# Sliding windows on one core: second halves of the split stores alternate with whole ones, and the copies without shuffle run on ScalarE

## Chip, cores, metric

One core of one Trainium2 chip. The metric is device time in microseconds (us) of one execution, as the median of several; all runs told here are in the fast state (one core, granted clock 1.0 in every profile). The profile's span is about 2 us shorter than the device time; where a sum is made from the profile, it is compared with the span. The sets of runs were made on different chips, so each is compared with the kernel before in its own rounds (196.74 to 197.01 us).

## The reference

```python
x: float32 [16, 64, 64, 64]; window_size = 8; stride = 4      # batch, c, h, w
n_h = n_w = 15
for i in range(n_h):
    for j in range(n_w):
        result[:, i, j] = x[:, :, 4*i : 4*i + 8, 4*j : 4*j + 8]   # [16, 64, 8, 8]
# result: float32 [16, 15, 15, 64, 8, 8]
```

Nothing is computed. 16.8 MB are read and 59 MB are written.

## The kernel before

x lies in one tile `L` with 128 partitions: 16 batches x 2 channel halves x 4 bands of 16 rows. A "window" in the code is one column position `j` and one row position `s` of a band, for all 128 partitions together. It is gathered into a slot of the ring `G` and stored by an indirect DMA that GpSimd (POOL) issues, since the output rows are scattered. For `s == 3` half of the rows come from the next band; a shuffle brings them over. The first 12 windows are stored in two halves of 16 channels, so that stores can begin when half of x is loaded.

```python
    UNITS = 18                                   # half slots in the ring
    G = gpool.tile([P, UNITS * HCL, WS, WS], f32, name="G")
    def window(j, s, half):
        ...
        g = G[:, u * HCL : (u + n) * HCL, :, :]
        if not last:
            nc.vector.tensor_copy(out=g, in_=L[:, cs, s * ST : s * ST + WS, cols])
        else:
            nc.vector.tensor_copy(out=g[:, :, 0:ST, :], in_=L[:, cs, s * ST : RB, cols])
            nc.vector.stream_shuffle(out=g[:, :, ST:WS, :], in_=L[:, cs, 0:ST, cols], mask=nxt)
        ...
        st = nc.gpsimd.indirect_dma_start(out=o, out_offset=..., in_=g..., ...)

    order = [(j, s) for j in range(NW) for s in range(NSLOT)]     # 60 windows
    EARLY = 12
    for half in range(2):
        for j, s in order[:EARLY]:
            window(j, s, half)
    for j, s in order[EARLY:]:
        window(j, s, None)
```

That makes 24 half stores and 48 whole ones. `idx_h` and `idx_hlast` in the profile are the halves, `idx` and `idx_last` the whole ones, "last" being those with a shuffle.

## Time and profile before

| | before |
|---|---|
| median (lowest to highest) | 196.94 us (196.81 to 197.00) |
| span of the profile | 194.9 us |
| DMA engines busy, 65 to 75 us | 0.83 |
| rate, 65 to 75 us | 338 GB/s |
| rate, 100 to 175 us | 409 GB/s |
| POOL from the first second-half store to the first whole one | 20.5 us, 1.71 us a store |

How to read it: the DMA engines are full in nearly every slice, so the time is bytes over rate, plus every stretch in which they have nothing to do. Between the start and the end there is one such stretch. The lines that show it stand in the prediction below. A line in order of time has the start and the duration in us, the engine, the line of the code, the operation and what it writes and reads; in brackets stand the engine's idle time before it and what ended that ("issue": nothing that the profile shows).

### The profile page before, as it was taken

The numbers are of one execution on the slowest core, as the hardware profiler recorded it, in microseconds if no ns is written. First come the engines' busy times: TensorE is split into PE (matmuls) and PEld (weight loads), VectorE is DVE, ScalarE is ACT, GpSimd is POOL, SyncE is SP. The second block draws the span as 40 slices with busy tenths as digits, with TensorE's granted clock in tenths as the row PEclk, the third lists the DMA queues.
The fourth block names the chain that finished last, engine by engine and source line by source line (L and its number), as shares of the span: only waits on it lengthen the run. The fifth ranks groups of instructions, "written<-read, shape, count | busy, mean of one in ns | idle before, by whom it ended". The sixth has DMA issues, their size and how long they took to land.

```text
span 194.9 us, 458 instructions
## 1 busy us (share of the span) xinstructions
DVE 85.7 (44%) x119; POOL 91.1 (47%) x77
## 2 busy tenths in 40 slices
DVE  2000069100699865464646464747474737430000
POOL 0000037723388888888854545454545454530000
DMA  5999999999999889999999999999999999999970
GB/s 182 419 401 415 409 409 414 423 420 419 419 415 421 353 334 387 403 414 398 403 409 405 414 405 407 410 403 412 407 414 407 412 409 409 409 407 419 422 298 20
DMA packets 14723, 75.79 MB, mean 389 GB/s; under 512 B 1984, under 2 KB 1984, under 8 KB 8960
## 3 DMA queue, kind: packets, MB, share of 16 engines
q0 software_dynamic: 10368, 58.99, 74.7%
q1 hardware_dynamic: 2176, 8.39, 10.9%
q10 hardware_dynamic: 2176, 8.39, 10.6%
q14 instruction: 3, 0.02, 0.0%
HBM read 16.78 MB, written 62.91 MB: 409 GB/s over the span
## 4 chain that ended last, share of the span: by engine, by line
DMA 52%; issue 28%; POOL 8%; POOLq 1%; PEldq 0%
DMA out_dram<-G,idx_last 38%; DMA out_dram<-G,idx_hlast 15%; POOL out_dram L109 8%; POOLq L158 1%; POOLq L109 0%; POOL pi L61 0%; PEldq L158 0%
## 5 line engine op out<-in xcount | busy, mean ns | idle before, releaser
L101 DVE COPY G<-L 128x2048 f32<-128x2048 f32 (+1 forms) x54 | 55.8, 1055 | 69.5 <-DMA L<-in_x_dram 39.5
L109 POOL DMA_INDIRECT out_dram<-G,idx x36 | 44.8, 1244 | 31.8 <-DMA out_dram<-G,idx 27.4
L109 POOL DMA_INDIRECT out_dram<-G,idx_h x18 | 22.5, 1250 | 37.8 <-DVE G L101 28.8
L109 POOL DMA_INDIRECT out_dram<-G,idx_last x12 | 16.7, 1392 | 8.9 <-DVE G L104 7.7
L104 DVE STREAM_SHUFFLE G<-L 128x1024 f32<-128x1024 f32 (+1 forms) x18 | 19.6, 1088 | 0.0
L103 DVE COPY G<-L 128x1024 f32<-128x1024 f32 (+1 forms) x18 | 11.6, 643 | 16.0 <-DMA out_dram<-G,idx 14.4
L109 POOL DMA_INDIRECT out_dram<-G,idx_hlast x6 | 6.8, 1130 | 3.7 <-DMA out_dram<-G,idx_hlast 2.5
L62 DVE TENSOR_SCALAR tb<-pi 128x1 int32<-128x1 int32 x1 | 0.2, 154 | 1.0 <-POOL pi L61 1.0
L61 POOL IOTA pi<- 128x1 int32 x1 | 0.1, 119 | 0.4 <-PEq L158 0.4
L104 DVE LOAD_MASK_SELECT G<-L x18 | 0.2, 12 | 0.0
L144 POOL MEMSET const-float32-0.0<- 128x1 f32 x1 | 0.1, 98 | 0.2 <-issue 0.2
L68 DVE CUSTOM_DVE_ANT_0 idx<-tb,tc 128x2 uint16<-128x2 uint16 x1 | 0.2, 160 | 0.0
L66 DVE CUSTOM_DVE_ANT_0 tb<-tb,tc 128x2 uint16<-128x2 uint16 x1 | 0.2, 159 | 0.0
L67 DVE TENSOR_SCALAR tc<-tq 128x1 int32<-128x1 int32 x1 | 0.2, 154 | 0.0
L77 DVE TENSOR_SCALAR idx_hlast<-idx_last 128x1 int32<-128x1 int32 x1 | 0.2, 154 | 0.0
L77 DVE TENSOR_SCALAR idx_h<-idx 128x1 int32<-128x1 int32 x1 | 0.2, 154 | 0.0
L71 DVE CUSTOM_DVE_ANT_0 idx_last<-idx,tq 128x2 uint16<-128x2 uint16 x1 | 0.2, 153 | 0.0
L65 DVE TENSOR_SCALAR tb<-tb 128x1 int32<-128x1 int32 x1 | 0.1, 149 | 0.0
L70 DVE TENSOR_SCALAR tq<-tq 128x1 int32<-128x1 int32 x1 | 0.1, 148 | 0.0
L63 DVE TENSOR_SCALAR tc<-pi 128x1 int32<-128x1 int32 x1 | 0.1, 145 | 0.0
L64 DVE TENSOR_SCALAR tq<-pi 128x1 int32<-128x1 int32 x1 | 0.1, 144 | 0.0
L144 POOL MEMSET const-uint8-127<- 128x1 uint8 x1 | 0.1, 118 | 0.0
(2 smaller groups left out, 0.2 us busy)
## 6 DMA issues: line engine op xcount, KB each, us to landing
L<-in_x_dram SPq DMA_DIRECT2D x8, 1024.0 KB, 19.9
L<-in_x_dram ACTq DMA_DIRECT2D x8, 1024.0 KB, 21.3
out_dram<-G,idx POOLq DMA_INDIRECT x36, 18.7
out_dram<-G,idx_h POOLq DMA_INDIRECT x18, 8.7
out_dram<-G,idx_last POOLq DMA_INDIRECT x12, 18.5
out_dram<-G,idx_hlast POOLq DMA_INDIRECT x6, 8.9
```

The lines of the kernel that those rows point to most:

```text
L62: nc.vector.tensor_scalar(out=tb[:, :], in0=pi[:, :], scalar1=3, scalar2=None, op0=ALU.logical_shift_right)
L66: nc.vector.tensor_tensor(out=tb[:, :], in0=tb[:, :], in1=tc_[:, :], op=ALU.add)
L67: nc.vector.tensor_scalar(out=tc_[:, :], in0=tq[:, :], scalar1=float(NSLOT * NW * CH), scalar2=None, op0=ALU.mult)
L68: nc.vector.tensor_tensor(out=idx[:, :], in0=tb[:, :], in1=tc_[:, :], op=ALU.add)
L71: nc.vector.tensor_tensor(out=idx_last[:, :], in0=idx[:, :], in1=tq[:, :], op=ALU.add)
L77: nc.vector.tensor_scalar(out=d[:, :], in0=e[:, :], scalar1=2.0, scalar2=None, op0=ALU.mult)
L101: nc.vector.tensor_copy(out=g, in_=L[:, cs, s * ST : s * ST + WS, cols])
L103: nc.vector.tensor_copy(out=g[:, :, 0:ST, :], in_=L[:, cs, s * ST : RB, cols])
L104: nc.vector.stream_shuffle(out=g[:, :, ST:WS, :], in_=L[:, cs, 0:ST, cols], mask=nxt)
L109: st = nc.gpsimd.indirect_dma_start(out=o, out_offset=bass.IndirectOffsetOnAxis(ap=ix[:, 0:1], axis=0), in_=g.rearrange("p c r w -> p (c r ...
L144: nc = _bacc.Bacc("TRN2", target_bir_lowering=False, num_devices=1)
L158: with _tile.TileContext(nc) as tc:
```

## The change

Its intent has two parts. POOL's issue costs the same for half a store as for a whole one, so halves in a row may feed the DMA too slowly; mixed with whole stores they need not. And copies on DVE can block POOL while it writes descriptors; on ScalarE they should not.

```diff
         if not last:
-            nc.vector.tensor_copy(out=g, in_=L[:, cs, s * ST : s * ST + WS, cols])
+            nc.scalar.copy(out=g, in_=L[:, cs, s * ST : s * ST + WS, cols])
...
-    for half in range(2):
-        for j, s in order[:EARLY]:
-            window(j, s, half)
-    for j, s in order[EARLY:]:
-        window(j, s, None)
+    for j, s in order[:EARLY]:
+        window(j, s, 0)
+    late = list(order[:EARLY])
+    rest = list(order[EARLY:])
+    while late:
+        for w in late[:2]:
+            window(*w, 1)
+        for w in rest[:2]:
+            window(*w, None)
+        late, rest = late[2:], rest[2:]
+    for w in rest:
+        window(*w, None)
```

## The prediction

> **What bounds the kernel now.** The kernel computes nothing: 16.8 MB of x come in, windows are gathered from tile L into the ring G, and 72 indirect stores, issued by GpSimd (POOL), write 59 MB out. So I read the page's slices first, for the one resource that carries all this.
>
> ```profile
> DVE 85.7 (44%) x119; POOL 91.1 (47%) x77
> DVE  2000069100699865464646464747474737430000
> POOL 0000037723388888888854545454545454530000
> DMA  5999999999999889999999999999999999999970
> GB/s 182 419 401 415 409 409 414 423 420 419 419 415 421 353 334 387 403 414 398 403 409 405 414 405 407 410 403 412 407 414 407 412 409 409 409 407 419 422 298 20
> ```
>
> One slice is 194.9/40 = 4.87 us. The DMA row is full from the second slice to the last but one, DVE and POOL are under half busy. The transfers are the bound, except in three slices, 13 to 15 (63 to 78 us), where the rate falls to 353, 334 and 387 GB/s. Next I read stretches around that place:
>
> ```profile
> core 0: us, DVE busy (x) POOL busy (x), PEclk, DMA share, GB/s
> 0.00:65.00 65.00, 24.42 (x54) 23.76 (x26) 1.00 0.99 398
> 65.00:75.00 10.00, 6.36 (x7) 8.17 (x7) 1.00 0.83 338
> 75.00:80.00 5.00, 2.12 (x3) 4.09 (x4) 1.00 0.98 395
> 80.00:100.00 20.00, 11.29 (x13) 15.94 (x13) 1.00 1.01 405
> 100.00:175.00 75.00, 41.46 (x46) 39.14 (x31) 1.00 1.01 409
> 175.00:186.00 11.00, 0.00 (x0) 0.00 (x0) 1.00 1.01 416
> 186.00:194.90 8.90, 0.00 (x0) 0.00 (x0) 1.00 0.33 138
> ```
>
> From 65 to 75 us the DMA engines are busy 0.83 of the time and POOL is occupied nearly without a break (8.17 busy, the rest mostly its 0.30 us between issues). GB/s times us is KB, so the bytes not moved there, against the steady 409, are (409-338)x10 + (409-395)x5 + (409-405)x20 = 710+70+80 = 860 KB, which is 860/409 = **2.1 us**. That is all that lies there to be had. Then I read the order of time, to see who is late:
>
> ```profile
> 35.55 0.96 POOL L109 DMA_INDIRECT out_dram<-G,idx_h  x1 [0.30 <-issue]
> 36.82 0.97 POOL L109 DMA_INDIRECT out_dram<-G,idx_hlast  x1 [0.30 <-issue]
> ...
> 51.54 1.16 POOL L109 DMA_INDIRECT out_dram<-G,idx_h  x1 [2.65 <-DVE G L101]
> ...
> 64.48 2.41 DVE L101 COPY G<-L 128x2048 f32<-128x2048 f32 x2
> 64.52 2.50 POOL L109 DMA_INDIRECT out_dram<-G,idx_h  x1 [0.30 <-DMA out_dram<-G,idx_h]
> ...
> 72.07 0.97 POOL L109 DMA_INDIRECT out_dram<-G,idx  x1 [0.30 <-issue]
> ```
>
> Undisturbed, a store costs POOL 0.97+0.30 = 1.27 us (35.55 to 36.82), whether half or whole. The issue at 64.52 took 2.50 us, exactly while two copies ran back to back on DVE. The twelve second-half stores start at 51.54, the first whole one at 72.07: 20.53/12 = 1.71 us each.
>
> **What the Trainium skill says.** "SBUF — State Buffer", section "Who interferes with whom": VectorE copies in a two-port mode and GpSimd take a shared SBUF port pair as an exclusive lock, and the loser waits for the whole instruction. That is the trap its section "SBUF: two separate sides" describes for descriptors written by GpSimd. The trace agrees: 0.96 us without a copy beside it, 2.50 us beside two. The first section also says that ScalarE never waits on anyone; nothing runs on ScalarE yet, so no trace shows it. "ScalarE: Activation LUTs", section "What ACT_TABLE_LOAD costs", gives 186 ns + 0.833 ns per element with immediate operands, and about 1.28 us for a table load (2.66 with the drain). My estimates from that page are 0.186+0.833x2.048 = 1.89 us for a whole copy and 1.04 us for a half one; DVE takes 1.24 and 0.69. "DMA: Bandwidth & Descriptors", section "Where 436 GB/s comes from", puts the ceiling of the 16 engines at 435 GB/s; the best stretches here reach about 420, so outside the dip little is left.
>
> **The change, part by part.** No bytes, stores or semaphores are added or removed. There are two parts.
>
> First part, the **order**. A half store moves 128 x 4096 B = 0.524 MB, and the shuffled quarter of them (s = 3, where one quarter of the partitions is masked) 0.393 MB. At the 418 GB/s of 50 to 65 us (slices 10 to 12 show 419, 415, 421) that is 1.25 and 0.94 us, on average 1.18 us. POOL needs 1.27 us undisturbed and 1.71 us as it was, so twelve halves in a row starve the DMA at any POOL speed, once what was queued is gone. How much is queued? L's last load lands near 50.5 us (the copy that waits for it starts at 50.57). By then the slices have moved about 19.8 MB. Loads and the twelve first halves together are 16.78 + 9x0.524 + 3x0.393 = 22.7 MB, so 2.9 MB are left, or 6.8 us. The DMA then has 6.8 + 12x1.18 = 21.0 us of work and would run dry at 71.5 us. POOL finishes issuing the halves only at about 71.8 and each still has to be transferred: a shortage of the order of the 2.1 us read above.
>
> Mixed, two groups alternate. Group A (two halves, two whole) is 3.15 MB, 7.5 us of DMA; POOL 4x1.27 = 5.1 us; ScalarE 2x1.04 + 2x1.89 = 5.9 us. Group B (a half, a shuffled half, a whole, a shuffled whole of 0.786 MB) is 2.75 MB, 6.6 us of DMA; POOL 5.1 us; ScalarE 2.9 us, DVE the rest. The suppliers are faster than the DMA in both. The lead is smallest at the start: first copy done at 50.6+1.04 = 51.6, store issued by 52.7, while the queue lasts to 57.4. The lead of 4.7 us only grows from there. So the dip goes: **-2.1 us**.
>
> Second part, the **engine**. In steady state four windows carry 3x1.049+0.786 = 3.93 MB, at 409 GB/s 9.6 us. ScalarE needs 3x1.89 = 5.7 us of it, DVE 0.69+1.28 = 2.0 us, POOL 5.1 us. All hidden. A slot of G is out of use for 1.89+1.27 instead of 1.24+1.27 us, 0.65 us more, against a median of 18.7 us from issue to landing. Hidden as well. At the start ScalarE's queue still issues x loads: its last one goes out at about 25.9 us and takes 0.65 us, so its first copy starts near 26.6 instead of 26.1, and a table load, if there is one, adds 1.3 to 2.7 us. The loads keep the DMA full until 50 us whichever store starts when, so I book **0 to +0.2 us**.
>
> Sum: 196.94 - 2.1 + 0.1 = **194.9 us**.
>
> **The rivals.**
> 1. *The dip isn't on the path.* The figures are means over 16 engines, and the end is set by the slowest of them. At 186 to 195 us the share is 0.33 because some finish about 3.5 us before the others. If the late ones had work in the dip, the gain would be under 1 us and the time 196 to 197. Against it: each store's landing is counted by 16 engine increments, and the last of the 16 also comes late in the dip. I find the four last halves taking about 6.1 us instead of 4.7, and some 0.5 us more in the stores after. So about 1.9 us of the 2.1 hold for the late engines too.
> 2. *The copies on DVE hold the DMA back everywhere*, and their move gives more than the dip: 409 GB/s in steady state, 416 after the last issue. If all of that came from DVE, 75 us x (1-409/416) = 1.3 us more, 193.6. Against it: I compared the durations of single 8 KB packets between 100 and 173 us. Beside a DVE copy alone they take 315 ns, beside nothing 316, beside POOL's issuing alone 335. It is POOL's issuing that costs, and that stays. This gets a small chance.
> 3. *ScalarE becomes a new wait*: copies half as long again, in order, behind its own load issues. At 5.7 of 9.6 us it would have to be 1.7 times slower than the estimate to bind. If the table load stood before its loads, the ramp would lose at most half the rate for 1.3 us, +0.6, that is 195.5. If it bound the mixed stage, the dip would come back: 196.5.
> 4. *The order was enough or not enough.* If POOL still takes 1.7 us beside nothing (no lock after all), a group takes it 6.8 us against 6.6 to 7.5 of DMA: still about even, with 4.7 us of lead. Time 195 to 195.5.
>
> **Range and chances.** Centre 194.9. Rival 1 with weight one in seven, and half of rivals 3 and 4, stretch it up to 196.2; part of rival 2 stretches it down to 194.0. Two per cent faster would be below 193.0, and that needs 3.9 us, more than the dip and all of rival 2 together. Two per cent slower is above 200.9 and needs ScalarE to bind the whole store stage. So within 2%: 0.95, faster 0.03, slower 0.02.
>
> **What would show it.** Right, step by step: no slice between 60 and 80 us under 395 GB/s; POOL issues of about 0.96 us beside ScalarE's copies, with no 2.5 us ones; ScalarE's copies at 1.9 and 1.0 us; steady state still 405 to 412 GB/s; the tail as ragged as now. It is wrong if the dip is gone and the time is not (rival 1), if the steady rate changes by over 1% (rival 2), or if POOL waits longest for ScalarE's copies (rival 3).

## The result

| | before | changed |
|---|---|---|
| median (lowest to highest) | 196.94 us (196.81 to 197.00) | 194.30 us (194.17 to 194.44) |
| span of the profile | 194.9 us | 192.4 us |
| ratio, 95% interval | | 0.9867 (0.985 to 0.9884) |

A ratio is the mean time of one kernel's fast runs over that of the other's of the same rounds, so it is not quite the ratio of the medians. The kernel is 2.6 us faster, which is inside 2%.

The slices of the changed kernel's page (busy tenths of 40 equal slices, and the rate):

```profile
DVE  2000050000232302303030122121121203030000
ACT  0000049500699875373747465646565655600000
POOL 0000027723367766456363253434343434440000
DMA  5999999999999999999999999999999999999960
GB/s 183 418 413 410 410 410 414 417 417 422 420 421 427 429 414 429 404 403 418 412 409 409 419 404 409 416 405 409 409 412 409 409 411 412 407 409 414 424 257 17
```

The three weak slices are gone; of slices 12 to 15, three now have the highest rates of the whole kernel (427 to 429 GB/s). The same stretches as shown before (columns: stretch and length, busy us of each engine with the number of instructions, clock, DMA share, GB/s):

```profile
core 0: us, DVE busy (x) ACT busy (x) POOL busy (x), PEclk, DMA share, GB/s
65.00:75.00 10.00, 2.29 (x4) 8.00 (x6) 6.49 (x7) 1.00 1.02 425
75.00:80.00 5.00, 1.43 (x4) 1.90 (x1) 1.96 (x3) 1.00 1.00 410
80.00:100.00 20.00, 3.99 (x9) 11.29 (x6) 10.66 (x12) 1.00 1.02 410
100.00:175.00 75.00, 14.47 (x22) 39.86 (x21) 28.96 (x30) 1.00 1.01 410
```

Between 65 and 100 us it moves (425-338)x10 + (410-395)x5 + (410-405)x20 = 870+75+100 = 1045 KB more than before. At 410 GB/s that is 2.5 us, the whole difference of the spans. From 100 to 175 us nothing changed (409 and 410), though DVE's work there fell from 41.5 to 14.5 us.

The costliest groups (busy us, mean ns of one | idle time before them and what ended most of it) and two of POOL's waits (us in total, times, longest):

```profile
L101 ACT COPY G<-L 128x2048 f32<-128x2048 f32 x36 | 68.0, 1898 | 40.6 <-DMA out_dram<-G,idx 18.6 <-DMA out_dram<-G,idx_last 10.6 <-DVE G L104 8.0
L109 POOL DMA_INDIRECT out_dram<-G,idx_h x18 | 17.4, 966 | 13.9 <-DMA out_dram<-G,idx_hlast 4.3 <-issue 3.8 <-ACT G L101 3.4
...
POOL out_dram L109 <- DMA out_dram<-G,idx: 44.6, 28, 2.3
...
POOL out_dram L109 <- ACT G L101: 5.6, 8, 2.7
```

POOL's issues take 0.97 us now where they took 1.25, and POOL waits for landings of earlier stores far more than for ScalarE.

### The profile page after: what moved, and what is told of

Same layout as the page of the kernel before. It is cut to its first block, busy times and chain, and to the rows that moved or that the text cites. A ratio compares the mean times of both kernels' runs of the same rounds, so it can differ in the third digit from the quotient of the medians.

```text
span 192.4 us, 478 instructions
## 1 busy us (share of the span) xinstructions
DVE 30.4 (16%) x65; ACT 86.2 (45%) x55; POOL 70.3 (37%) x77
## 3 DMA queue, kind: packets, MB, share of 16 engines
HBM read 16.78 MB, written 62.91 MB: 414 GB/s over the span
## 4 chain that ended last, share of the span: by engine, by line
DMA 65%; issue 19%; ACT 3%; POOL 1%; POOLq 1%; PEldq 0%
DMA out_dram<-G,idx_last 38%; DMA out_dram<-G,idx 14%; DMA out_dram<-G,idx_h 8%; DMA out_dram<-G,idx_hlast 6%; ACT G L101 3%; POOL out_dram L109 1%; POOLq L165 1%; POOLq L109 0%; POOL pi L61 0%; PEldq L165 0%
## 5 line engine op out<-in xcount | busy, mean ns | idle before, releaser
L101 ACT COPY G<-L 128x2048 f32<-128x2048 f32 (+1 forms) x54 | 84.9, 1613 | 54.4 <-DMA out_dram<-G,idx 18.6
L109 POOL DMA_INDIRECT out_dram<-G,idx x36 | 34.8, 966 | 47.0 <-DMA out_dram<-G,idx 43.1
L103 DVE COPY G<-L 128x1024 f32<-128x1024 f32 (+1 forms) x18 | 11.1, 618 | 138.3 <-DMA out_dram<-G,idx 62.8
L109 POOL DMA_INDIRECT out_dram<-G,idx_h x18 | 17.4, 966 | 13.9 <-DMA out_dram<-G,idx_hlast 4.3
L109 POOL DMA_INDIRECT out_dram<-G,idx_hlast x6 | 5.9, 990 | 27.9 <-DVE G L104 26.4
L109 POOL DMA_INDIRECT out_dram<-G,idx_last x12 | 11.8, 986 | 11.7 <-DVE G L104 6.8
L101 ACT ACT_TABLE_LOAD x1 | 1.3, 1283 | 26.6 <-DMA L<-in_x_dram 26.6
```

What stands on the lines that cost most here:

```text
L101: nc.scalar.copy(out=g, in_=L[:, cs, s * ST : s * ST + WS, cols])
L109: st = nc.gpsimd.indirect_dma_start(out=o, out_offset=bass.IndirectOffsetOnAxis(ap=ix[:, 0:1], axis=0), in_=g.rearrange("p c r w -> p (c r ...
```

## The experiments

A quantity that separates them is the pace at which POOL gets the second halves out. For kernels in the old order I take the time from the first second-half issue to the first whole one, divided by the number of halves: 20.53/12 = 1.71 us before. The DMA needs 1.18 us for one on average.

### Order alone

The changed kernel with its copies back on DVE:

```diff
-            nc.scalar.copy(out=g, in_=L[...])
+            nc.vector.tensor_copy(out=g, in_=L[...])
```

> The new order with all copies left on DVE. Theory A (the order is what counts: whole stores feed the DMA while POOL works): the dip is gone, about 194.5 us, no slice between 60 and 80 us under 400 GB/s, though single POOL issues still take 1.5 to 2.5 us beside the copies. Theory B (POOL freed of the port lock is what counts): POOL still needs some 1.7 us per store, 6.8 us per group of four stores against 6.6 to 7.5 us of DMA; part of the dip stays, 195.5 to 196.5 us.

Measured: 194.65 us (before, in the same rounds: 196.74), ratio 0.9890 (0.9874 to 0.9907). In order of time, and by stretch:

```profile
59.61 3.11 DVE L101 COPY G<-L 128x2048 f32<-128x2048 f32 x3
60.23 2.00 POOL L109 DMA_INDIRECT out_dram<-G,idx_hlast  x1 [0.30 <-issue]
...
65.00:75.00 10.00, 6.70 (x10) 7.87 (x8) 1.00 1.03 427
```

POOL is blocked as before, 2.00 us for an issue beside copies, and the dip is gone all the same. The slow issues do no harm once whole stores lie among them. Theory A holds for the order.

### Engine alone

The old order, with the copies without shuffle on ScalarE:

```diff
-            nc.vector.tensor_copy(out=g, in_=L[...])
+            nc.scalar.copy(out=g, in_=L[...])
```

> The old order with the copies on ScalarE. Theory A, as the prediction has it (twelve halves in a row starve the DMA at any POOL speed): a dip stays, near 196 us. Theory B (POOL at 1.27 us per half needs 15.2 us for twelve, and the 6.8 us queued when the loads end cover the 1.1 us that this is over the DMA's 14.1): no dip at all, about 194.4 us, the same as the whole change.

Measured: 194.28 us, ratio 0.9873 (0.9857 to 0.989): as much as the whole change.

```profile
65.00:75.00 10.00, 1.89 (x3) 6.29 (x5) 7.71 (x8) 1.00 1.03 422
...
L109 POOL DMA_INDIRECT out_dram<-G,idx_h x18 | 17.4, 968 | 13.7 <-DMA out_dram<-G,idx_hlast 4.7 <-ACT G L101 3.5 <-issue 3.0
```

With issues of 0.97 us the halves go out one every 1.28 us. Twelve take 15.3 us against 14.1 us of DMA, and the queue left by the loads covers the difference. So each part alone takes the dip away, and the two gains don't add.

### Is it the port or the busy engine?

The old order, the copies still on DVE, but as a maximum over one element, which writes the same values and, by the section on interference that the prediction cites, never contends for the shared pair on this chip:

```diff
-            nc.vector.tensor_copy(out=g, in_=L[...])
+            src = L[...].rearrange("p c r (w one) -> p c r w one", one=1)
+            nc.vector.tensor_reduce(out=g, in_=src, op=ALU.max, axis=mybir.AxisListType.X)
```

> The old order, copies on DVE as a maximum over one element, an instruction that by the Trainium skill never takes the shared port pair[...]. If the lock is the cause of the slow POOL issues: POOL issues near 0.97 us, and the time within 0.5 us of the run with the copies on ScalarE in the old order. If a slow POOL is due to DVE being busy in any way: POOL issues stay above 1.2 us on average and the dip stays, near 197 us.

Measured: 194.45 us, ratio 0.9881 (0.9865 to 0.9898).

```profile
65.00:75.00 10.00, 10.00 (x8) 5.89 (x7) 1.00 1.03 422
...
L102 DVE TENSOR_REDUCE G<-L 128x2048 f32<-128x2048 f32 x36 | 80.7, 2279 | 2.6 <-DMA out_dram<-G,idx 2.2
L110 POOL DMA_INDIRECT out_dram<-G,idx_h x18 | 17.6, 977 | 38.9 <-DVE G L102 30.0 <-DMA out_dram<-G,idx_h 5.2 <-issue 3.7
```

DVE is now busy for all of the ten microseconds, slower by 1.8 times per copy, and POOL's issues take 0.98 us; the halves go out every 1.27 us. So it is not DVE being busy that slows POOL, but this form of copy. That a port lock is the reason is the skill's account; these runs agree with it and don't show the lock itself. ScalarE isn't needed for the gain.

### Which copies block POOL

Two halves of the engine change, both in the old order: only the half copies on ScalarE, then only the whole copies.

```diff
-            nc.vector.tensor_copy(out=g, in_=L[...])
+            if half is not None:                 # second run: if half is None
+                nc.scalar.copy(out=g, in_=L[...])
+            else:
+                nc.vector.tensor_copy(out=g, in_=L[...])
```

> Old order, only the 18 half copies on ScalarE. In the profile before, POOL's issues of the second halves were over 0.97 us by 0.9 us in total beside half copies, and by 4.3 us beside whole copies that run ahead. Theory (whole copies running ahead are what blocks POOL): most of the dip stays, 195.5 to 196.5 us. Rival (any relief of POOL or DVE is enough): 194.3 us.

> Old order, only the 36 whole copies on ScalarE. Theory (whole copies running ahead are what blocks POOL): no dip, 194.2 to 194.6 us. Rival (the half copies beside their own stores block POOL as much): a dip stays, over 195.3 us.

Measured, before at 197.01 us: half copies moved, 195.44 us, 0.9917 (0.9901 to 0.9934); whole copies moved, 194.09 us, 0.985 (0.9834 to 0.9867). Of the first, in order of time and by stretch, then the same stretch of the second:

```profile
54.50 1.23 DVE L105 COPY G<-L 128x2048 f32<-128x2048 f32 x1 [0.24 <-DMA out_dram<-G,idx_h]
54.86 1.70 POOL L113 DMA_INDIRECT out_dram<-G,idx_hlast  x1 [0.30 <-issue]
...
65.00:75.00 10.00, 5.46 (x6) 0.00 (x0) 7.94 (x7) 1.00 0.95 384
```

```profile
65.00:75.00 10.00, 1.89 (x3) 5.82 (x4) 7.56 (x9) 1.00 1.03 424
```

With the half copies moved, part of the dip stays (384 GB/s, DMA share 0.95) and a half costs POOL 1.63 us; with the whole copies moved the dip is gone and a half costs 1.38 us. So it is mainly the copies of whole windows, which run ahead on DVE while the second halves still wait to be issued, that hold POOL up: moving them saves 0.33 us a half, moving the half copies 0.08 us. The time does not divide in the same way. The expectation that most of the dip stays was wrong: 195.44 us is just under its range, and of the 710 KB missing between 65 and 75 us, only (409-384)x10 = 250 KB are missing still. The next section has a reason.

### How the queue decides

Two runs change the number of split windows: 24 with all copies without shuffle on ScalarE (old order), and 8 with only the whole copies there.

```diff
-    EARLY = 12
+    EARLY = 24                                   # second run: EARLY = 8
```

> Old order, copies on ScalarE, 24 windows in halves, so 24 second halves in a row. By the count of issues (POOL 24 x 1.27 = 30.5 us against 24 x 1.18 = 28.2 us of DMA, a deficit of 2.2 us under a queue of at least 6.8 us): no dip. By the prediction's sentence that halves in a row starve the DMA at any POOL speed: a dip after the halves. With 12 stores more, at 0.2 us each, 196.5 us; if the cost per store holds only late in the kernel, 194.3 us.

> As e7 (old order, whole copies on ScalarE), but only 8 windows in halves: four stores fewer. If each store that is issued costs the DMA some 0.2 us (e8 issued 18 more and took 3.7 us longer): 193.3 us. If the queue at the end of the loads is then too short (12 halves left 2.9 MB, 8 leave some 0.9 MB, 2.2 us, against the 3.3 us that copy, issue and way take): a gap of about 1 us near 50 us, which eats this: 194 to 194.6 us.

Measured, before at 196.89 us: 24 split, 196.86 us, 1.0001 (0.9986 to 1.0016); 8 split, 197.61 us, 1.003 (1.0016 to 1.0044). The stretches of the kernel with 24, then those of the kernel with 8:

```profile
65.00:75.00 10.00, 2.27 (x7) 6.84 (x7) 7.70 (x8) 1.00 1.03 415
...
90.00:100.00 10.00, 1.91 (x3) 5.86 (x4) 7.56 (x9) 1.00 1.02 389
```

```profile
50.00:55.00 5.00, 4.55 (x9) 4.59 (x3) 2.97 (x3) 1.00 0.88 355
55.00:60.00 5.00, 3.17 (x7) 5.00 (x4) 3.78 (x5) 1.00 0.87 352
60.00:65.00 5.00, 1.93 (x3) 2.59 (x2) 3.78 (x5) 1.00 0.92 358
```

With 24 halves in a row, from 65 to 96 us, the DMA share is 1.00 or more in every stretch of 2 us: no starving. It is slow all the same, because its packets take longer (see the next run). With 8 the queue is short: when the loads end, some 1.0 MB is left (19.7 MB moved of 16.78 + 6x0.524 + 2x0.393 = 20.7), 2.3 us, and the first new store comes only then. After that the DMA runs at POOL's pace: a half is 0.491 MB on average and goes out every 1.38 us, and 0.491/1.38 = 356 GB/s is close to what the three lines show, though the first still holds the rest of the queue and the last the first whole stores. My expectation for this run was too mild, a gap of 1 us; it starved for all eight halves.

So both parts of the argument are needed: halves in a row supply too little at either pace, and whether that is felt depends on what is queued when they start.

The prediction's own sum tells the kernels apart. By it the DMA has work until 71.5 us; the last half should be through by then, so its issue has to end 1.18 us before. My estimate, from the end of that issue in each trace:

| old order, on ScalarE | pace of a half | last half issued by | with 1.18 us, against 71.5 us | missing, 65 to 75 us, at 409 GB/s |
|---|---|---|---|---|
| nothing (before) | 1.71 us | 71.8 us | 1.5 us late | 1.7 us |
| half copies | 1.63 us | 70.3 us | even | 0.6 us |
| whole copies | 1.38 us | 67.6 us | 2.7 us early | none |
| both | 1.28 us | 66.0 us | 4.3 us early | none |

The sum leaves out the way from issue to transfer, and what is missing lies some 0.3 to 0.6 us above it. So a small gain in pace is worth much of the dip, and a POOL that is earlier than needed gains nothing more here. It is a sum made after the runs, and no run was made to test it.

### More halves, all through

The changed kernel, with every second of the remaining windows in halves:

```diff
-    for w in rest:
-        window(*w, None)
+    for k, w in enumerate(rest):
+        if k % 2:
+            window(*w, None)
+        else:
+            window(*w, 0)
+            window(*w, 1)
```

> The changed kernel with every second of the remaining windows stored as two halves (rows of 4 KB in place of 8 KB). The spread between the first and last engine of a store stays near 0.6 us as long as many half stores are in the queue and grows to 4.4 us with whole ones alone. If the size of the pieces is the cause: spread at the end under 3 us, 412 to 418 GB/s from 100 to 175 us, 192.5 to 193.7 us. If it is only the time that the store stage lasts: spread and rate as before, 194.3 us. POOL needs 3 x 1.27 = 3.8 us for two windows against 4.9 us of DMA, so POOL should not bind.

Measured: 197.98 us (before 197.01), ratio 1.0051 (1.0034 to 1.0068); slower than the changed kernel, against both expectations.

```profile
100.00:175.00 75.00, 15.62 (x24) 41.15 (x35) 43.34 (x45) 1.00 1.02 399
```

The DMA share is 1.02 and the rate is 399 GB/s, not 410: the engines are full and each packet takes longer. In the trace's packet records, 8 KB packets of stores take 309 ns on average until about 75 us and 325 to 326 ns from 100 us on (322 in the kernel before), 4 KB packets 159 ns and then 168 to 169. The spread between the first and the last of the 16 engines of one store is 5.8 us at the end here, 4.4 us in the changed kernel and 3.5 us before. My idea that small pieces keep the engines together is wrong. More stores go with slower packets: 18 more cost 3.7 us here, and 12 more cost 2.6 us in the run with 24 split windows. Part of that is the size alone, as two 4 KB packets of 159 ns take 318 ns where one of 8 KB takes 309. Whether POOL's descriptor writing is what slows the packets these runs don't settle, nor why it begins between 70 and 76 us in most kernels; it began near 60 us in the kernel with 8 split windows.

### Stores without POOL

To see the DMA without POOL's descriptors, I cut every store of the order-alone kernel into plain transfers of 32 partitions, issued by the sync and scalar queues:

```diff
-        st = nc.gpsimd.indirect_dma_start(...)
+        for q in range(HQ - 1 if last else HQ):
+            eng = (nc.sync, nc.scalar)[...]      # in turn
+            st = eng.dma_start(out=ov[:, q * NSLOT + s, j], in_=gf[q::HQ, :])
```

> The new order, copies on DVE, every store cut into four plain transfers of 32 partitions issued by the sync and scalar queues: POOL issues nothing. If POOL's descriptor work makes half of the DMA engines late (the end spread of 4.4 us between the first and the last engine of one store): the spread falls under 1 us, steady rate 415 to 420 GB/s instead of 410, about 190 to 192 us. If not: spread and rate stay, 194 to 196 us, or worse where the issue (0.6 us each, two queues, 1.2 us per window and queue) or the smaller pieces cost.

Measured: 468.83 us. One of DVE's waits (us in total, times, longest) tells why:

```profile
DVE G L101 <- DMA out_dram<-G: 261.8, 53, 19.0
```

The copies waited for the stores just before them; I put it down to the strided slices of the one tile G, which made copies and stores run one after the other. The run says nothing about POOL. Mended with one tile per slot:

```diff
-    G = gpool.tile([P, UNITS * HCL, WS, WS], f32, name="G")
+    Gs = [gpool.tile([P, 2 * HCL, WS, WS], f32, name=f"G{k}") for k in range(UNITS // 2)]
```

> As e4, but with a tile of its own for each of the nine slots of G, so that a copy waits for its own slot's stores only; e4's copies waited for the stores just before them, and its 469 us say nothing about POOL. If POOL's descriptor work makes half of the DMA engines late: end spread under 1.5 us and 415 to 420 GB/s in steady state, 190 to 193 us. If POOL has no part in it: spread of 4 us stays, 194 us or more. If eight transfers of 0.25 MB in flight are too few to cover the way there and back: below 380 GB/s, over 205 us.

Measured: 239.02 us, ratio 1.214 (1.2106 to 1.2175).

```profile
100.00:175.00 75.00, 35.83 (x43) 0.00 (x0) 1.00 0.91 315
```

The rate is 315 GB/s at a share of 0.91, with 8 KB packets of 355 and 392 ns on average from the two queues. That is the third case of the expectation (below 380 GB/s, over 205 us), though no run shows whether too few transfers in flight or their shape is the cause. The last store's spread is 1.8 us, between the first two cases. As this kernel has a limit of its own, the question whether POOL makes the packets slow stays open.

### The better split of the work

Since only the whole copies need to leave DVE's two-port form, the kernel of that run was set beside the changed one in the same rounds, both unchanged:

> The changed kernel once more, beside the next one: 194.3 us.

> Old order, only the whole copies on ScalarE, once more beside the changed kernel. If it is better: 0.1 to 0.3 us below it. If the difference of 0.2 us was chance: the same.

Measured: changed kernel 194.35 us (194.31 to 194.41), ratio 0.9871; old order with the whole copies alone on ScalarE 193.98 us (193.89 to 194.19), ratio 0.9856. The two sets of runs don't overlap, so the simpler edit is ahead by 0.4 us (0.2%) here; the earlier medians, 194.09 and 194.30 us, point the same way but come from different rounds. It is the fastest version. Its last store shows a smaller spread of the engines, 3.9 us against 4.6; that fits the gain, but no run shows that it is the cause.

## Why the prediction was right, and where it was not

**What bounds the kernel.** Right. The time fell by what the DMA moved more between 65 and 100 us, 2.5 us of span.

**The size of the dip.** 2.1 us were predicted, 2.6 came. The term of the sum that was mis-sized is the rate that takes the place of the dip. I measured the missing bytes against the steady 409 GB/s, 710 KB for the ten microseconds from 65 us; the changed kernel moves 425 GB/s there, 870 KB more. There an 8 KB packet takes 309 to 310 ns on average and a 4 KB one 159, against 322 for 8 KB in the steady stage.

**"First part, the order", -2.1 us, and "second part, the engine", 0 to +0.2 us.** This split is the step that fails. The engine alone gives 194.28 us, all of the gain; the order alone gives 194.65. The sentence that led there, that "twelve halves in a row starve the DMA at any POOL speed, once what was queued is gone", is true (8 split windows showed it at a short queue) but was applied where its condition isn't met: at 1.27 us a half POOL lags by 12x(1.27-1.18) = 1.1 us, and 6.8 us were queued. The prediction had both numbers and did not set them against each other: it put its 71.5 us beside the issues of the slow POOL alone. At 1.27 us a half the last issue would end at 51.54 + 12x1.27 - 0.30 = 66.5 us, 5 us before the DMA runs dry.

**The lock.** Right as far as the runs show it. POOL's mean issue of a half fell from 1.25 to 0.97 us on ScalarE; with a one-port instruction on DVE it was 0.98. In POOL's pace, the whole copies running ahead, not the half ones, did most of it. The lock itself is the skill's account of this and is not seen in a trace.

**ScalarE's cost.** Right: 1898 and 1042 ns a copy where 1.89 and 1.04 us were estimated. The table load took 1.28 us. It stood behind the load issues, so that rival 3's case of a table load ahead of them didn't occur. In order of time:

```profile
26.59 1.28 ACT L101 ACT_TABLE_LOAD   x1 [26.59 <-DMA L<-in_x_dram]
26.97 0.41 DVE L103 COPY G<-L 128x512 f32<-128x512 f32 x1
...
27.36 1.12 POOL L109 DMA_INDIRECT out_dram<-G,idx_hlast  x1 [26.41 <-DVE G L104]
27.88 8.62 ACT L101 COPY G<-L 128x1024 f32<-128x1024 f32 x9
```

The first store is issued at 27.36 us (27.09 before), ahead of ScalarE's first copy, since the shuffled halves, which need no ScalarE, were put in front of the others.

**The rivals.** The dip was on the path (rival 1 falls: the time followed the bytes). Copies on DVE don't hold the steady stage back (rival 2 falls: 409 and 410 GB/s). ScalarE is no new wait (rival 3 falls: 5.6 us of POOL's waits in all, against 44.6 for landings). Rival 4, the order with POOL as slow as before, was put at 195 to 195.5 us and measured 194.65 (beside 196.74 for the kernel before), a little too cautious.

**The tail.** I expected it as ragged as before. It is slightly worse, 4.4 us of spread instead of 3.5.

## What to carry to other kernels

When a queue feeds the bound resource, set the pace of each supplier against the drain together with what is queued when the slow stretch begins; a supplier that is too slow costs nothing until the queue is gone. When a change has two parts that serve one stretch, ask of each whether it would be enough alone: gains for the same gap don't add, and the smaller edit may be the better kernel. With stores issued by GpSimd, look at copies that run ahead on VectorE: they need not be on any path to hold the stores up.

## What the Trainium skill lacked or had wrong

- "SBUF — State Buffer", section "Who interferes with whom": nothing is missing here. It does not list the stream shuffle by name, but its rule for DVE instructions outside the two-port modes can be read to cover it, and the trace agrees. In the kernel before, a whole shuffle from 102.61 to 103.90 us and a POOL issue from 102.67 us ran side by side, and the issue took its 0.96 us: the shuffle doesn't block it. What the section says of copies (issues up to 2.50 us) and reductions (0.98 us beside a DVE that was never idle) is confirmed.
- "ScalarE: Activation LUTs", section "What ACT_TABLE_LOAD costs": the load took the section's 1283 ns, and the copy formula agrees to within 10 ns. The drain that the section adds for about 2.66 us in total was not seen here: the first copy began at 27.88 us, 0.01 us after the load's end. The section speaks of a switch to another set; this was the kernel's first and only load, so that case is not tested.
- "DMA: Bandwidth & Descriptors", section "Issuing engine by pattern", says that transfers from the sync and scalar queues are generally faster. Stores of 32 strided partitions there reached 315 GB/s in steady state, indirect ones of 128 partitions from GpSimd 409 to 410. As size and shape differ, this is an exception to the sentence and no like comparison of the issuing engines.
- "DMA: Bandwidth & Descriptors", section "Latency and other measured facts", names engines 7 and 15 as the usually slower ones. Here eight of the 16 engines fall behind the other eight together during a long row of stores, by 3.5 to 5.8 us at the end. The trace does not number them, so whether 7 and 15 are among them is not known. No page I read has it that store packets of 8 KB go from 309 to some 322 ns after about 70 to 76 us. The cause of both is open.
